# Pairing small matmuls on row halves, ending the norms' square sums on TensorE, and moving two low parts to VectorE

## The chip, the cores and the metric

The kernel runs on one core of a Trainium2 chip. The metric is the device time of one execution, in microseconds (us), as a median of runs; smaller is better. PE is TensorE (PEld its weight loads), DVE is VectorE, ACT is ScalarE, POOL is GpSimd, SP is SyncE.

## The reference, cut to what matters

256 tokens of width 1024 pass through two stacks of two layers. Everything is float32.

```python
def first_block(x, p, ...):
    for i in range(2):
        z = rmsnorm(x, norm_mix[i]) @ w_in[i]        # 14 pieces: queries, keys, values, gates ...
        y_a = nsa_mixer(...) @ w_up_nsa[i]           # compressed, selected and sliding-window keys
        y_b = retention(...) @ w_up_ret[i]
        x = x + (sigmoid(merge_a) * y_a + sigmoid(merge_b) * y_b) @ w_out[i]
        x = x + square(relu(rmsnorm(x, norm_mlp[i]) @ w_ff1[i])) @ w_ff2[i]
        x = x + sigmoid(rmsnorm(x, norm_ple[i]) @ w_ple_gate[i]) * (p[i] @ w_ple[i])

def rmsnorm(x, g):
    return x * rsqrt(mean(x * x, axis=-1) + 1e-6) * g

def second_block(x, ...):
    # layer 0: mixer_sb_ssm, then an MLP; layer 1: mixer_dsa, then an MLP; a layer norm behind each
    ...

def mixer_sb_ssm(x, w_in, ...):
    q, k, v, u = split(x @ w_in)                     # 8 heads of 64; u: 32 groups of 16 channels
    a_out = stick_breaking_attention(q, k, v)        # z = q k / 8; log sigmoids; a cumulative sum over keys
    y = s5_ssm(u, ...)                               # bu = u @ bbar (complex, 64 states a group), a scan, c @ x
    ...
    return concat(a_out, y) @ w_out
```

## The kernel before, in words

Each product of activations and weights is made of three fp32r matmuls: a high part times a high part, and each high part times the other's low part (`mm3`, L388 to L390; `paired`, L438 and L440, does it in two). Weights come in by DMA from one packed array (`raw`), ACT rounds them to the high part `hi` (L363) and DVE or POOL subtracts to get the low part `lo` (L366). The table `POOL` at the head of `_Env` says for which weight names POOL makes the first low part of a key; "ksw", the selected and sliding keys of the first stack, is in it, but only for layer 1 (`_split`).

A program writer issues the work in stages, with generators at the side (`_Env.add`, `step`, `run`): each step of the main work lets every generator in the side list take one step, up to its next `yield`. A scheduler then orders the instructions of each engine. It simulates a time line and may place an instruction of a later stage ahead of or between others; `e.behind((ins,))` keeps what stands in it behind an instruction. So the order on an engine isn't the order of the program text. PSUM banks come from two pools of four, "a" and "w"; a matmul that wants a bank has to wait until the reader of the bank's earlier use is through.

The parts that the change touches:

- **Norms** (`_Norm`; six of them in the first stack: mixer, MLP and PLE norm of each layer). The activations stand transposed, channels on partitions. For each of four slices of two channel groups, ACT squares 128x512 values (L516), and POOL (DVE for the first norm) adds them to a sum (L520); with slice 3 the two halves of the sum are folded into one (L522). `stats` then multiplies the 128x256 sum with a matrix of minus ones: two program matmuls of two columns, one for each half of the tokens (L532), which sums over the partitions. DVE and POOL's power function turn that into the factor `rc`, and a later matmul (L551) spreads it as `rb`. The products with the weights don't wait for it: the factor is applied when the results are read. In the PLE stage, POOL also scales x by `rb2` in four pieces (L694), and `stats` waits one step before its matmuls are issued.
- **Stick-breaking scores** (`stage_a`, `stage_b`, `side_attention` in `_second`). Heads 2j and 2j+1 stand on rows 0 to 63 and 64 to 127 of `kT` and `qT`. For one head at a time, `stage_a` multiplies a mask by a unit matrix into a bank (L1324, 128 rows), then two products of 64 rows (L1325, L1327); ACT makes three passes and DVE one (L1333). `stage_b` of the head before adds cumulative sums to the same bank (L1338, L1340, L1342).
- **State space inputs** (`_ssm_run`, L1887). For k = 0 to 3 and four quarters q, two program matmuls on 64 rows (rows 0 to 63 for even q, 64 to 127 for odd q) write one bank; DVE rotates it by cosines and sines, POOL combines, DVE scans. It is a generator at the side; it yields behind every second quarter.

## Time and profile before

| | |
|---|---|
| median of 3 runs | 1476.12 us (1475.64 to 1477.32) |
| profiled execution | 1473.14 us, of which the span is 1471.4 us |
| mean granted clock of TensorE | 0.993 of full speed |
| PE busy | 1435.8 us, 98% of the span |
| PEld busy | 1269.1 us |
| DVE, ACT, POOL busy | 1090.3, 784.9, 274.5 us |

The span runs from the first to the last instruction; 1.74 us of the profiled execution lie around it. PE's matmuls are pipelined, so that their busy times overlap; what one costs is read from the start of one to the start of the next. A row of the time line is: start, busy time, engine, line, operation, output and inputs, and in brackets the idle time before it with what ended it. "x4" in such a row means four machine instructions in a run; a float32 matmul (not fp32r) is two instructions for one of the program.

### The profile page before, as it was taken

To read this page: it belongs to the slowest core of one execution; us is meant where nothing else is said; L and a number is where in the kernel's file an instruction comes from. 1 tells how busy PE (TensorE), PEld (TensorE's weight loads), DVE (VectorE), ACT (ScalarE), POOL (GpSimd) and SP (SyncE) were. 2 spreads that over 40 slices of the span, in tenths; PEclk is the share of its full clock that TensorE was granted. 3 is DMA by queue.
4 is the path that set the end of the run, shared out by engine and by line. 5 is a ranking of instruction groups with operands and counts; after the bars stand their busy time and mean duration, and the time that the engine had idled before them with its cause. 6 is when DMAs were issued, how large, how long until landed. Compare 5 with 4: busy or idle time off the path is not lost.

```text
span 1471.4 us, 24711 instructions
## 1 busy us (share of the span) xinstructions
PE 1435.8 (98%) x9636; PEld 1269.1 (86%) x9636; DVE 1090.3 (74%) x1820; ACT 784.9 (53%) x1258; POOL 274.5 (19%) x201
## 2 busy tenths in 40 slices
PE   9999999999999999999999999999999998999997
PEld 6878999999998779999999998778888796788886
DVE  7796669666678696679877778877666688686666
ACT  6665545444556564455645555365444465654442
POOL 2343314000045343213000337510000100100000
PEclk9999999999999999999999999999999998999999
DMA  8553555655546653555565453336556362366551
GB/s 291 188 179 109 173 172 177 198 186 187 178 146 195 198 172 130 173 166 191 188 198 180 154 185 122 101 129 216 192 181 198 123 220 75 100 208 193 186 190 69
DMA packets 70677, 250.66 MB, mean 170 GB/s; under 512 B 8096, under 2 KB 8480, under 8 KB 70560
## 3 DMA queue, kind: packets, MB, share of 16 engines
q1 hardware_dynamic: 70560, 249.07, 51.6%
q8 instruction: 76, 1.25, 0.3%
q14 instruction: 41, 0.34, 0.1%
HBM read 247.99 MB, written 1.05 MB: 169 GB/s over the span
## 4 chain that ended last, share of the span: by engine, by line
PE 49%; DVE 4%; issue 1%; ACT 1%; POOL 0%; DVEq 0%; POOLq 0%
PE psw L438 11%; PE psa L388 9%; PE psa L390 9%; PE psa L389 9%; PE psw L440 6%; DVE lo L366 1%; DVE b L1896 1%; PE psw L2033 1%; PE psw L389 0%; PE psw L2019 0%; PE psw L390 0%; ACT b L1607 0%; PE psw L1887 0%; PE psw L388 0%; DVE b L1984 0%
## 5 line engine op out<-in xcount | busy, mean ns | idle before, releaser
L366 DVE TENSOR_TENSOR lo<-raw,hi 128x1024 fp32r<-128x1024 f32 (+1 forms) x409 | 512.5, 1260 | 216.7 <-ACT hi L363 215.9
L363 ACT ACTIVATE hi<-raw 128x1024 fp32r<-128x1024 f32 (+1 forms) x448 | 465.7, 1047 | 386.8 <-issue 141.4
L438 PE MATMUL psw<-act,hi 128*128 128x512 f32 x960 | 340.7, 397 | 0.0
L440 PE MATMUL psw<-act,lo 128*128 128x256 f32 x960 | 268.0, 281 | 0.0
L438 PEld LDWEIGHTS psw<-act,hi 128*128 128x128 f32 x960 | 179.9, 188 | 41.0
L440 PEld LDWEIGHTS psw<-act,lo 128*128 128x128 f32 x960 | 181.5, 189 | 1.7
L390 PE MATMUL psa<-b,lo 128*128 128x256 f32 x640 | 180.5, 283 | 0.0
L389 PE MATMUL psa<-b,hi 128*128 128x256 f32 x640 | 180.2, 283 | 0.0
L388 PE MATMUL psa<-b,hi 128*128 128x256 f32 x640 | 177.8, 283 | 0.0
L388 PE MATMUL psa<-act,hi 128*128 128x256 f32 x456 | 132.2, 291 | 0.0
L390 PE MATMUL psa<-act,lo 128*128 128x256 f32 x456 | 130.3, 286 | 0.5 <-DVE lo L366 0.5
L389 PE MATMUL psa<-act,hi 128*128 128x256 f32 x456 | 130.8, 287 | 0.0
L366 POOL TENSOR_TENSOR lo<-raw,hi 128x1024 fp32r<-128x1024 f32 x39 | 96.0, 2461 | 173.7 <-ACT hi L363 158.9
L389 PE MATMUL psa<-lo,act 128*128 128x512 f32 (+2 forms) x320 | 121.6, 383 | 3.6 <-DVE lo L366 2.6
L388 PE MATMUL psa<-hi,act 128*128 128x512 f32 (+2 forms) x320 | 122.3, 390 | 1.6 <-ACT hi L363 1.2
L390 PEld LDWEIGHTS psa<-b,lo 128*128 128x128 f32 x640 | 122.1, 191 | 0.1
L389 PEld LDWEIGHTS psa<-b,hi 128*128 128x128 f32 x640 | 122.0, 191 | 0.0
L388 PEld LDWEIGHTS psa<-b,hi 128*128 128x128 f32 x640 | 120.5, 191 | 1.2
L390 PE MATMUL psa<-hi,act 128*128 128x512 f32 (+2 forms) x320 | 117.9, 382 | 0.0
L388 PE MATMUL psa<-hi,b 128*128 128x512 f32 x256 | 99.7, 391 | 0.0
L389 PE MATMUL psa<-lo,b 128*128 128x512 f32 x256 | 99.6, 390 | 0.0
L390 PE MATMUL psa<-hi,b 128*128 128x512 f32 x256 | 98.7, 389 | 0.0
(360 smaller groups left out, 2692.2 us busy)
## 6 DMA issues: line engine op xcount, KB each, us to landing
raw<-in_ws_dram SPq DMA_DIRECT2D x450, 512.0 KB, 4.1
b<-in_ln_dram SPq DMA_DIRECT2D x8, 512.0 KB, 5.1
raw<-in_ws_dram SPq DMA_DIRECT2D x8, 280.0 KB, 3.7
raw<-in_ws_dram SPq DMA_DIRECT2D x4, 264.0 KB, 2.7
b<-in_x_dram SPq DMA_DIRECT2D x4, 256.0 KB, 5.0
out_dram<-b SPq DMA_DIRECT2D x4, 256.0 KB, 2.0
cb<-in_cb_dram SPq DMA_DIRECT2D x1, 676.0 KB, 7.1
b<-in_p_dram SPq DMA_DIRECT2D x2, 256.0 KB, 5.0
```

The source lines that it names most:

```text
L363: self.nc.scalar.activation(out=hi, in_=w, func=AF.Copy)
L366: eng.tensor_tensor(out=lo, in0=w, in1=hi.bitcast(F32), op=ALU.subtract)
L388: mm(out=out, lhsT=lh, rhs=rh, start=start, stop=False, skip_group_check=shared)
L389: mm(out=out, lhsT=lh, rhs=rl, start=False, stop=False, skip_group_check=shared)
L390: self.mlast = mm(out=out, lhsT=ll, rhs=rh, start=False, stop=stop, skip_group_check=shared)
L438: mm(out=bank.rearrange("p (v t) -> p v t", v=2), lhsT=h[:, c], rhs=act[2][k], start=k == 0, stop=False, skip_group_check=True)
L440: mm(out=bank[:, :256], lhsT=l[:, c], rhs=act[0][k], start=False, stop=k == len(hi) - 1, skip_group_check=True)
L1896: V.tensor_tensor_scan(out=xs[:, q, c], data0=mt[:, q], data1=w[:, q, c], initial=0.0, op0=ALU.mult, op1=ALU.add)
L2033: PE.matmul(out=o[64 * gg:64 * gg + 64, q0:256], lhsT=vw[:, kt, v0:v0 + 64], rhs=pts[s - 1 + gg][:, 256 * kt:256 * kt + 256 - q0], start=k ...
```

## The change

Four edits.

1. "ksw" leaves the table `POOL`, so both low parts of these keys in layer 1 are made by DVE, as those of layer 0 were.
2. The squares of slice 3 are no longer added to the sum and the fold is gone. The sum of slices 0 to 2 and the squares of slice 3, each with two halves, are four operands for `stats`, which accumulates them with four matmuls for each half of the tokens: eight program matmuls of two columns instead of two. In the PLE stage `stats` waits two steps instead of one, and POOL's four scalings of x stand behind the last of the norm's adds.
3. `stage_a` takes both heads of a pair: the products of the two row halves alternate in two banks, the mask matmuls come last. `side_attention` issues the two `stage_b` behind it, one step later.
4. The state space inputs take two quarters together, on opposite row halves, alternating in two banks.

```diff
-    POOL = {"rv": 1, "rg": 1, "ma": 1, "mb": 1, "up": 1, "su": 1, "glu": 1, "sv": 1, "ksw": 1}
+    POOL = {"rv": 1, "rg": 1, "ma": 1, "mb": 1, "up": 1, "su": 1, "glu": 1, "sv": 1}
...
-            pool = n < self.POOL.get(key[0], 0) and key[:2] != ("ksw", 0)
-            eng = self.nc.gpsimd if pool else self.nc.vector
+            eng = self.nc.gpsimd if n < self.POOL.get(key[0], 0) else self.nc.vector
...
-        if self.sum is None:
-            self.sum = sq
+        if c in (0, 3):
+            self.sum = [self.sum, sq] if c else sq
         else:
-            eng.tensor_tensor(out=self.sum, in0=self.sum, in1=sq, op=ALU.add)
-        if c == 3:
-            eng.tensor_tensor(out=self.sum[:, 0], in0=self.sum[:, 0], in1=self.sum[:, 1], op=ALU.add)
+            self.added = eng.tensor_tensor(out=self.sum, in0=self.sum, in1=sq, op=ALU.add)
...
         for T in range(2):
-            PE.matmul(out=ps[:, 2 * T:2 * T + 2], lhsT=self.sum[:, 0, 128 * T:128 * T + 128], rhs=K["negones"][:, :2])
+            for n in range(4):
+                PE.matmul(out=ps[:, 2 * T:2 * T + 2], lhsT=self.sum[n // 2][:, n % 2, 128 * T:128 * T + 128],
+                          rhs=K["negones"][:, :2], start=n == 0, stop=n == 3)
...
-        st = norm.stats("a", rs["prior"], wait=1)
+        st = norm.stats("a", rs["prior"], wait=2)
         e.add(st)
-        for b in range(4):
-            k = slice(2 * b, 2 * b + 2)
-            G.tensor_tensor(out=xT[:, k], in0=xT[:, k], in1=rs["rb2"], op=ALU.mult)
+        with e.behind((norm.added,)):
+            for b in range(4):
+                k = slice(2 * b, 2 * b + 2)
+                G.tensor_tensor(out=xT[:, k], in0=xT[:, k], in1=rs["rb2"], op=ALU.mult)
...
-    def stage_a(s):
-        j, g = s // 2, s % 2
-        hs = slice(64 * g, 64 * g + 64)
-        ps = e.bank()
-        diag = ps[:, :].rearrange("p (a q) -> p a q", a=4)[:, 0:4:2]
-        PE.matmul(out=diag, lhsT=im[:, 0], rhs=smask2, start=True, stop=False, skip_group_check=True)
-        PE.matmul(out=ps[:, 0:256], lhsT=kT[hs, j, 0:128], rhs=qT[hs, j, :], start=False, stop=False,
-                  skip_group_check=True)
-        PE.matmul(out=ps[:, 256:384], lhsT=kT[hs, j, 128:256], rhs=qT[hs, j, 128:256], start=False, stop=False,
-                  skip_group_check=True)
...
+    def stage_a(j):
+
+        pss = [e.bank() for _ in range(2)]
+        for o, n in ((0, 128), (256, 256)):
+            for g in range(2):
+                hs = slice(64 * g, 64 * g + 64)
+                PE.matmul(out=pss[g][:, o:o + 384 - n],
+                          lhsT=kT[hs, j, n - 128:n], rhs=qT[hs, j, n - 128:256], start=o == 0, stop=False,
+                          skip_group_check=True)
+        for g in range(2):
+            diag = pss[g].rearrange("p (a q) -> p a q", a=4)[:, 0:4:2]
+            PE.matmul(out=diag, lhsT=im[:, 0], rhs=smask2, start=False, stop=False, skip_group_check=True)
...
     def side_attention():
-        ready, lag = [], 1
-        for s in range(8 + lag):
-            while s >= 4 and "qk" not in D:
+        ready = []
+        for j in range(4):
+            while j >= 2 and "qk" not in D:
                 yield
-            if s < 8:
-                stage_a(s)
-            if s >= lag:
-                stage_b(s - lag)
-                if (s - lag) % 2:
-                    ready.append((s - lag) // 2)
+            stage_a(j)
             yield
-            if ready and "v" in D:
-                stage_c(ready.pop(0))
+            for g in range(2):
+                stage_b(2 * j + g)
+                if ready and "v" in D:
+                    stage_c(ready.pop(0))
+            ready.append(j)
+            yield
...
         for q in range(4):
-            h = slice(64 * (q % 2), 64 * (q % 2) + 64)
-            ps = e.bank()[:, :256].rearrange("p (c j) -> p c j", c=2)
-            for c in range(2):
-                PE.matmul(out=ps[:, c], lhsT=S["bT"][h, c, 2 * k + q // 2], rhs=up[h, k, q // 2])
+            if q % 2 == 0:
+                pss = [e.bank()[:, :256].rearrange("p (c j) -> p c j", c=2) for _ in range(2)]
+                for c in range(2):
+                    for n in range(2):
+                        h = slice(64 * n, 64 * n + 64)
+                        PE.matmul(out=pss[n][:, c], lhsT=S["bT"][h, c, 2 * k + q // 2], rhs=up[h, k, q // 2])
+            ps = pss[q % 2]
```

Because lines move, L520 is L519 afterwards, L532 is L530, L1887 is L1892, and the first of three split matmuls (L388) is L387.

How the instructions of an engine stand in a row was compared at three places. First PE at the state space inputs. Names such as psw_10494 are PSUM banks, "x2" are two program matmuls in a run. Before, the last two quarters of k = 2 stood next to each other:

```order
L390 MATMUL psa_10469<-hi_10323,act_9765 128x512
L1887 MATMUL psw_10494<-b_1691_10035,b_1487_8648 128x128 x2
L1887 MATMUL psw_10505<-b_1691_10035,b_1487_8648 128x128 x2
L388 MATMUL psa_10468<-hi_10327,act_9773 128x512
L389 MATMUL psa_10468<-lo_10328,act_9773 128x512
L1324 MATMUL psw_10516<-b_1683_9995 128x2x128
L1325 MATMUL psw_10516<-b_1680_9992,b_1681_9993 128x256
L1327 MATMUL psw_10516<-b_1680_9992,b_1681_9993 128x128
```

Afterwards, the same quarters:

```order
L1892 MATMUL psw_10523<-b_1691_10059,b_1487_8668 128x128 x2
L387 MATMUL psa_10498<-hi_10356,act_9797 128x512
L388 MATMUL psa_10498<-lo_10357,act_9797 128x512
L389 MATMUL psa_10498<-hi_10356,act_9797 128x512
L387 MATMUL psa_10497<-hi_10356,act_9797 128x512
L388 MATMUL psa_10497<-lo_10357,act_9797 128x512
L1892 MATMUL psw_10524<-b_1691_10059,b_1487_8668 128x128 x2
L1342 MATMUL psw_10419<-b_1761_10431,cb_7527 128x256
```

Five matmuls of another product stand between the two quarters. Over all eight pairs, four are adjacent before and one afterwards; that one is followed by a head's scores:

```order
L1892 MATMUL psw_10255<-b_1691_10059,b_1487_8668 128x128
L1892 MATMUL psw_10256<-b_1691_10059,b_1487_8668 128x128
L1892 MATMUL psw_10255<-b_1691_10059,b_1487_8668 128x128
L1892 MATMUL psw_10256<-b_1691_10059,b_1487_8668 128x128
L1325 MATMUL psw_10277<-b_1680_10016,b_1681_10017 128x256
L1325 MATMUL psw_10277<-b_1680_10016,b_1681_10017 128x128
L1330 MATMUL psw_10277<-b_1683_10019 128x2x128
L387 MATMUL psa_10226<-act_9879,hi_10124 128x256
```

The other head of the pair (psw_10278) comes ten rows later; none of the four pairs of heads stands together.

Second, POOL at the PLE norm of layer 0 (b_5 is x, b_758 the sum of squares). Before:

```order
L694 TENSOR_TENSOR b_5_96<-b_5_96,b_514_2843 128x512
L520 TENSOR_TENSOR b_758_4519<-b_758_4519,b_760_4527 128x512
L694 TENSOR_TENSOR b_5_96<-b_5_96,b_514_2843 128x512
L520 TENSOR_TENSOR b_758_4519<-b_758_4519,b_762_4536 128x512
L694 TENSOR_TENSOR b_5_96<-b_5_96,b_514_2843 128x512
L520 TENSOR_TENSOR b_758_4519<-b_758_4519,b_764_4545 128x512
L694 TENSOR_TENSOR b_5_96<-b_5_96,b_514_2843 128x512
L522 TENSOR_TENSOR b_758_4519<-b_758_4519 128x256
L603 TENSOR_TENSOR rc_4668<-rc_4668,mhalf_128 128x2
```

Afterwards:

```order
L519 TENSOR_TENSOR b_758_4527<-b_758_4527,b_760_4535 128x512
L519 TENSOR_TENSOR b_758_4527<-b_758_4527,b_762_4544 128x512
L694 TENSOR_TENSOR b_5_96<-b_5_96,b_514_2851 128x512 x4
L602 TENSOR_TENSOR rc_4717<-rc_4717,mhalf_128 128x2
L519 TENSOR_TENSOR b_802_4825<-b_802_4825,b_805_4837 128x512
```

The adds now stand ahead of all four scalings, an add and the fold are gone, and the power function (L602) stands behind the scalings as before. On PE, the statistics of this norm stand 24 program matmuls of the gate's product later than before.

Third, PE at the first norm, while the first weights arrive (psa_213 to psa_216 are banks of the first product). Before, the statistics came 26 rows behind these:

```order
L390 MATMUL psa_215<-hi_148,act_152 128x280
L390 MATMUL psa_216<-hi_148,act_152 128x280
L388 MATMUL psa_215<-hi_167,act_157 128x280
L388 MATMUL psa_216<-hi_167,act_157 128x280
L389 MATMUL psa_215<-lo_168,act_157 128x280
```

Afterwards:

```order
L389 MATMUL psa_214<-hi_148,act_152 128x280
L530 MATMUL psw_291<-ones_64,b_27_178 128x2 x2
L530 MATMUL psw_291<-ones_64,b_30_186 128x2 x2
L530 MATMUL psw_291<-ones_64,b_27_178 128x2 x2
L530 MATMUL psw_291<-ones_64,b_30_186 128x2 x2
L387 MATMUL psa_213<-hi_167,act_157 128x280
L387 MATMUL psa_214<-hi_167,act_157 128x280
L388 MATMUL psa_213<-lo_168,act_157 128x280
```

The statistics moved in between two weight parts.

## Rows read from the trace of the kernel before

**Rows 1.** The page: span's busy times, and the group of DVE's low parts

```profile
PE 1435.8 (98%) x9636; PEld 1269.1 (86%) x9636; DVE 1090.3 (74%) x1820; ACT 784.9 (53%) x1258; POOL 274.5 (19%) x201
...
L366 DVE TENSOR_TENSOR lo<-raw,hi 128x1024 fp32r<-128x1024 f32 (+1 forms) x409 | 512.5, 1260 | 216.7 <-ACT hi L363 215.9
```

**Rows 2.** Waits of PE: total us, times, longest us

```profile
PE psa L532 <- POOL b L522: 4.0, 2, 2.1
...
PE psa L389 <- DVE lo L366: 2.6, 3, 1.7
PE psw L1338 <- DVE b L1333: 2.2, 3, 1.0
...
PE psa L389 <- POOL lo L366: 0.9, 1, 0.9
```

**Rows 3.** Time line of PE, an MLP norm's statistics; columns as told above

```profile
660.18 0.40 PE L438 MATMUL psw<-act,hi 128*128 128x512 f32 x1
660.42 0.28 PE L440 MATMUL psw<-act,lo 128*128 128x256 f32 x1
660.53 0.50 PE L532 MATMUL psw<-ones,b 128*128 128x2 f32 x4
660.90 0.48 PE L438 MATMUL psw<-act,hi 128*128 128x512 f32 x1
661.21 0.28 PE L440 MATMUL psw<-act,lo 128*128 128x256 f32 x1
```

**Rows 4.** Time line of PE, the PLE norm's statistics of layer 0

```profile
417.17 0.61 PE L532 MATMUL psa<-ones,b 128*128 128x2 f32 x4 [2.05 <-POOL b L522]
```

**Rows 5.** Time line of POOL ahead of those statistics

```profile
413.25 2.20 POOL L694 TENSOR_TENSOR b<-b,b 128x512 f32<-128x512 f32 x1 [1.95 <-DVE act L484]
415.42 1.70 POOL L522 TENSOR_TENSOR b<-b 128x256 f32<-128x256 f32 x1
```

**Rows 6.** Time line of PE, start of layer 1

```profile
440.47 0.50 PE L389 MATMUL psa<-lo,act 128*128 128x512 f32 x1 [0.94 <-POOL lo L366]
...
444.36 0.50 PE L389 MATMUL psa<-lo,act 128*128 128x512 f32 x1 [1.73 <-DVE lo L366]
```

**Rows 7.** Time line of POOL, start of layer 1

```profile
437.78 5.44 POOL L366 TENSOR_TENSOR lo<-raw,hi 128x1024 fp32r<-128x1024 f32 x2 [0.22 <-ACT hi L363]
```

**Rows 8.** Time line of DVE, start of layer 1

```profile
438.98 1.99 DVE L706 SCALAR_TENSOR_TENSOR b<-b,b 128x512 f32<-128x512 f32 x1
440.89 3.42 DVE L366 TENSOR_TENSOR lo<-raw,hi 128x1024 fp32r<-128x1024 f32 x1
```

**Rows 9.** Time line of PE near the start

```profile
10.70 0.29 PE L390 MATMUL psa<-hi,act 128*128 128x280 f32 x1
12.19 0.52 PE L388 MATMUL psa<-hi,act 128*128 128x280 f32 x2 [1.20 <-ACT hi L363]
13.37 0.40 PE L389 MATMUL psa<-lo,act 128*128 128x280 f32 x1 [0.66 <-DVE lo L366]
```

**Rows 10.** Time lines of DVE and ACT near the start

```profile
10.59 0.68 DVE L520 TENSOR_TENSOR b<-b,b 128x512 f32<-128x512 f32 x1
...
10.97 0.61 ACT L516 ACTIVATE b<-b 128x512 f32<-128x512 f32 x1
```

**Rows 11.** Two stretches: us, busy of PE, PEld, DVE, ACT, POOL; clock; DMA

```profile
13.92:17.33 3.41, 3.41 (x15) 3.21 (x15) 2.79 (x4) 1.51 (x2) 0.00 (x0) 0.50 1.03 403
...
885.00:945.00 60.00, 57.83 (x409) 47.40 (x408) 53.98 (x85) 28.21 (x45) 41.72 (x43) 1.00 0.31 99
```

**Rows 12.** Time line of PE, state space inputs: one quarter, then two adjacent

```profile
892.96 0.28 PE L390 MATMUL psa<-act,lo 128*128 128x256 f32 x1
893.17 0.71 PE L1887 MATMUL psw<-b,b 64*128 64x128 f32 x4
893.81 0.39 PE L388 MATMUL psa<-act,hi 128*128 128x256 f32 x1
894.03 0.28 PE L389 MATMUL psa<-act,hi 128*128 128x256 f32 x1
...
896.16 0.72 PE L1887 MATMUL psw<-b,b 64*128 64x128 f32 x8
896.81 0.38 PE L1324 MATMUL psw<-b 128*128 128x256 f32 x1
```

More of the change, by code (lines that the diff above doesn't have):

```diff
@@ L502, in __init__ @@
         self.K, self.g = K, g
-        self.sum = self.rc = self.rb = None
+        self.sum = self.rc = self.rb = self.added = None
     def slice(self, xT, c):
@@ L1317, in _second @@
     sc, ws = {}, {}
-    def stage_a(s):
-        j, g = s // 2, s % 2
-        hs = slice(64 * g, 64 * g + 64)
-        ps = e.bank()
-        diag = ps[:, :].rearrange("p (a q) -> p a q", a=4)[:, 0:4:2]
-        PE.matmul(out=diag, lhsT=im[:, 0], rhs=smask2, start=True, stop=False, skip_group_check=True)
-        PE.matmul(out=ps[:, 0:256], lhsT=kT[hs, j, 0:128], rhs=qT[hs, j, :], start=False, stop=False,
-                  skip_group_check=True)
-        PE.matmul(out=ps[:, 256:384], lhsT=kT[hs, j, 128:256], rhs=qT[hs, j, 128:256], start=False, stop=False,
-                  skip_group_check=True)
-        l = e.t("b2", [128, 384])
-        A.activation(out=l, in_=ps[:, :384], func=AF.Abs)
-        A.activation(out=l, in_=l, func=AF.Exp, scale=-1.0)
-        A.activation(out=l, in_=l, func=AF.Ln, bias=1.0)
-        V.scalar_tensor_tensor(out=l, in0=ps[:, :384], scalar=0.0, in1=l, op0=ALU.max, op1=ALU.add)
-        sc[s] = (ps, l)
+    def stage_a(j):
[10 more added lines that the diff above has]
+        for g in range(2):
+            ps = pss[g]
+            l = e.t("b2", [128, 384])
+            A.activation(out=l, in_=ps[:, :384], func=AF.Abs)
+            A.activation(out=l, in_=l, func=AF.Exp, scale=-1.0)
+            A.activation(out=l, in_=l, func=AF.Ln, bias=1.0)
+            V.scalar_tensor_tensor(out=l, in0=ps[:, :384], scalar=0.0, in1=l, op0=ALU.max, op1=ALU.add)
+            sc[2 * j + g] = (ps, l)
     def stage_b(s):
@@ L1362, in side_attention @@
     def side_attention():
-        ready, lag = [], 1
-        for s in range(8 + lag):
-            while s >= 4 and "qk" not in D:
+        ready = []
+        for j in range(4):
+            while j >= 2 and "qk" not in D:
                 yield
-            if s < 8:
-                stage_a(s)
-            if s >= lag:
-                stage_b(s - lag)
-                if (s - lag) % 2:
-                    ready.append((s - lag) // 2)
-            yield
-            if ready and "v" in D:
-                stage_c(ready.pop(0))
+            stage_a(j)
+            yield
+            for g in range(2):
+                stage_b(2 * j + g)
[3 more added lines that the diff above has]
+            yield
         while ready:
```

## The prediction

> **What bounds the kernel now.** I read the page's busy times first: PE is busy 1435.8 us of a span of 1471.4 us and no other engine comes near it [rows 1]. So the order of PE's instructions and the few places where PE stands still decide the time, and a part of the change counts by what it does to PE's steps. Next I read the list of what PE waited for [rows 2]. Four of its entries lie where the change works: the square sums' statistics wait for the folded sum on POOL twice, 4.0 us in all; weight parts waited for DVE 2.6 us and once for POOL 0.9 us; the second stage of the stick-breaking scores (L1338) waited three times, 2.2 us. Then I read the time line of PE at each place, where a row "x4" is four machine instructions of two program matmuls: an fp32 matmul is two instructions, and the time from one row's start to the next one's is what it costs PE. All sums below stand against the profiled execution, 1473.14 us; the three timed runs have a median of 1476.12 us, 2.98 us more, and I carry the difference of the sum over to the median.
>
> **Statistics of the norms, the price.** Before, a norm has two L532 matmuls, four instructions; now eight, sixteen instructions. In a stretch without a wait four take 0.37 us from 660.53 to 660.90, and the next L438 takes 0.31 us (660.90 to 661.21) where an ordinary one takes 0.24 us (660.18 to 660.42) [rows 3]: 0.44 us in all, 0.11 us each. Twelve more per norm are 12 x 0.11 = 1.33 us, and 8.0 us for six norms if nothing hides them. The Trainium skill ("TensorEngine Tiling (Array Packing)", section Instruction Overhead) says that a matmul has about 60 cycles of overhead, so that one column lasts as long as sixty; that would be 0.025 us for each of these two-column instructions, an estimate from that page, and 0.3 us instead of 1.33 us for the twelve. The row disagrees, 0.11 us each, with a 128x128 weight load in every one. Statistics that cost next to nothing are rival C.
>
> **MLP norms (two).** The sums are ready: adds and statistics stand in a stretch where PE does not wait [rows 3]. Nothing hides the 1.33 us there. Term: 2 x 1.33 = **+2.7 us**; +2.3 if each hides one 0.2 us step's worth of waiting that I don't see.
>
> **PLE norms (two).** PE idles 2.05 us ahead of L532, until POOL's fold L522 has ended [rows 4]; the second norm has the same wait (2 times, 4.0 us in all [rows 2]). On POOL the fold comes last, behind a 2.20 us scaling of x (L694) and itself 1.70 us [rows 5]. Now only two adds stand ahead of the statistics, the four scalings are behind them, the fold is gone, and the order puts 24 more program matmuls ahead of the statistics on PE. So the wait goes; what is late next is the last square on ACT, and that stands ahead of those 24 matmuls. The added 1.33 us stays, since it fills PE itself. POOL's power function on the statistics is now queued behind all four scalings, but POOL has an add and the 1.70 us fold less to do, so they end before 415.45, where the last scaling ended before [rows 5], and PE comes to the statistics only after that. Term: 2 x (1.33 - 2.03) = **-1.4 us**; if the wait came back behind the scalings, up to +2.7.
>
> **Mixer norm of layer 1 and the two sliding-key low parts.** At 440.47 PE waits 0.94 us for POOL's low part and at 444.36 again 1.73 us for DVE's [rows 6]. On POOL the two low parts take 5.44 us [rows 7], and beside them DVE is slow: 3.42 us for a low part whose mean is 1.26 us [rows 1], and 1.99 us for an L706 [rows 8]. With both low parts on DVE, POOL is quiet, DVE has 2 x 1.26 = 2.5 us more to do and wins back 3.42 - 1.26 = 2.2 us and a part of the 1.99 us. I take half of the 2.67 us of waits to remain, since DVE is still the one that hands PE its low parts here one after the other. Term: 1.33 - 1.4 = **-0.1 us**, between -1.4 (all waits gone) and +1.3 (all there).
>
> **Startup norm.** PE idles 1.20 us before 12.19 and 0.66 us before 13.37 [rows 9]. In the new order the sixteen instructions stand in that wait: the last needed add on DVE ends at 11.27 and the last square on ACT at 11.58 [rows 10], so they run from 11.3 to about 13.1. The two L388, 0.52 us busy together, then end their steps near 13.55 and L389 starts there instead of at 13.37, 0.18 us later; the four at 18.3 are gone, 0.44 us. That is -0.3 us. Behind the waits the granted clock fell to half (1.2 instead of 2.4 GHz) from 13.92 to 17.33, 3.41 us [rows 11], which costs half of that, 1.7 us. PE stood nearly still for 1.86 of the 3 us before; now it has statistics there. Waits of 2 us elsewhere [rows 4] were followed by no fall, so the rows don't settle whether it falls again; I take half. Term: -0.3 - 0.8 = **-1.1 us**, between +0.2 and -2.1.
>
> **State space inputs.** An isolated quarter (x4) costs PE, from 892.96 to 894.03, 1.07 us less the 0.24 us of the two matmuls around it, **0.83 us**; two quarters on opposite row halves that stand next to each other (x8) take 0.65 us from 896.16 to 896.81, where one alone takes 0.64 from 893.17 to 893.81 [rows 12]. So the second quarter of an adjacent pair is free. The code before issues quarter after quarter, but its order already has four of eight pairs adjacent; the changed code asks for pairs, but its order has one adjacent pair, and in seven the scheduler put other matmuls between the quarters. Groups to pay for: before 4 + 8 = 12, now 1 + 14 = 15. Term: 3 x 0.83 = **+2.5 us**; +1.5 if quarters beside other half-row matmuls save their way in or out.
>
> **Scores.** No two heads stand next to each other in the new order either; each head is two products on 64 rows and then the mask matmul. The same three matmuls cost the same. Twice a head follows directly on a quarter of the state space inputs, which are 64 rows too, and one way out and one way in (0.10 us each, the excess of 0.21 and 0.22 over 0.12 around x4 in [rows 12]) fall away: **-0.4 us**, between 0 and -0.6. The three waits of stage b, 2.2 us [rows 2], I leave as they are: the rows between a head's scores and its L1342 number 22 to 71 now, 23 to 71 before.
>
> **Sum**: +2.7 - 1.4 - 0.1 - 1.1 + 2.5 - 0.4 = **+2.2 us**, so 1475.3 us for a profiled execution like the one shown and **1478.3 us** for the median. A measurement here can tell about 0.2%, 2.95 us, from no change; so this is "same", nearer to the slower end. With its terms at their near bounds the forecast reaches from 1475 to 1481 us.
>
> **Rivals.**
>
> A. The waits all go: startup keeps its clock (-2.1), the layer boundary waits no more (-1.4), the stage b waits end because both heads' scores come early (-2.2), and the quarters save their ways (+1.5). With +2.7 - 1.4 - 0.6 the sum is -3.5 us: **1472.6 us**. For it: each of these waits has its releaser on DVE or POOL, which lose work there. Against it: four things must come together. Chance 0.22.
>
> B. Stage b becomes late. Both heads' scores are asked for at once, so six ACT passes and two DVE steps stand one after another, and the second head's L1342 comes while DVE, busy 53.98 of 60 us in this stretch [rows 11], is still behind; two scores and two quarters now hold all four banks of their pool until DVE has read them. It decides from the point where the PE work between a head's score and its L1342 is shorter than that chain, about 25 rows. Price: if all eight heads wait the longest wait seen, 1.0 us [rows 2], 8.1 us instead of 2.2, +5.9 us, the sum is +8.1: **1484.2 us**. For it: the waits exist already at 23 to 27 rows. Against it: the scheduler spread the heads. Chance 0.18.
>
> C. The twelve added instructions of a norm take PE no time, because their weight loads run beside the work ahead. Then 1.33 us goes from the terms of the MLP norms, the PLE norms and the boundary, five times, 6.7 us: sum -4.5 us, **1471.6 us**. The Trainium skill's overhead figure above points this way. The 0.37 us of four [rows 3] speaks against it. Chance 0.02. That the pairs really run as pairs, -3.3 instead of +2.5, would take another order than the one built; I give it no more than is in C.
>
> **How the numbers follow.** The forecast has 0.58, and of it 0.13 lies above 1479.07, the bound of slower; B adds 0.18, so slower has 0.31, same 0.45, and faster, from A and C, 0.24. The range reaches down to A and up towards B: 1472.5 to 1482.5 us; about 2 in 10 lie outside, most of them above.
>
> **What would show it.** Right: L530 in bursts of 0.11 us without idle time ahead of it at both PLE norms; one x8 and fourteen x4 groups of L1892, each x4 at 0.83 us; no POOL low part at the second layer's start and PE's waits there shorter than 2.67 us. Wrong: waits for L1342 of more than 4 us in all (B); a granted clock that stays full near 14 us together with no wait at the layer boundary and at L1342 (A); sixteen L530 in far less than 1.7 us (C).

## The result and the profile after

The changed kernel takes **1484.5 us** (median of 5 runs, 1480.8 to 1487.0), the kernel before 1476.1 us (5 runs, 1473.2 to 1477.3): ratio 1.0054, 95% interval 1.0037 to 1.0070. It is slower by 8 us; the forecast was 1478.3 us with a range up to 1482.5.

The profiled execution of the changed kernel took 1484.52 us, its span is 1482.7 us. It stands at the median, that of before stood 3 us under its own, so between the two traces lie 11.3 us. Both traces hold the same 8040 split matmuls (`mm3` and `paired`). The start of the n-th one after, less its start before, is how far the change has fallen behind by then:

| stretch (start in the trace before) | forecast, us | measured, us |
|---|---|---|
| startup, to 58 us | -1.1 | -0.5 |
| attention of layer 0, 70 to 82 us | 0 | +2.5, later -0.2 |
| two MLP norms (234, 662 us) | +2.7 | +1.0 and +1.0 |
| first PLE norm (417 us) | -0.7 | -1.0 |
| start of layer 1 (436 to 460 us) | -0.1 | -0.1 |
| attention of layer 1 | 0 | +0.3 |
| second PLE norm (848 us) | -0.7 | -0.9 |
| start of the second stack (867 to 869 us) | 0 | +1.5 |
| state space mixer and stick-breaking heads (881 to 978 us) | +2.1 | **+6.8** |
| the rest | 0 | +1.1 |

The PLE norms and the start of layer 1 went nearly as told, the MLP norms cost less. The time line of PE at the first norm answers [rows 9]; then the first PLE norm answers [rows 4], and the start of layer 1 [rows 6]:

```profile
11.27 1.95 PE L530 MATMUL psw<-ones,b 128*128 128x2 f32 x16 [0.33 <-DVE b L519]
13.08 0.50 PE L387 MATMUL psa<-hi,act 128*128 128x280 f32 x2
...
420.46 1.84 PE L530 MATMUL psa<-ones,b 128*128 128x2 f32 x16
422.17 0.36 PE L387 MATMUL psa<-act,hi 128*128 128x256 f32 x1
...
443.42 0.50 PE L388 MATMUL psa<-lo,act 128*128 128x512 f32 x1 [0.28 <-DVE lo L365]
445.29 0.40 PE L387 MATMUL psa<-hi,act 128*128 128x280 f32 x1 [0.44 <-ACT act L482]
```

Sixteen statistics take 1.71 us from 420.46 to 422.17, 0.107 us each; nothing waits ahead of them any more; at the start they run from 11.27 to 13.08, and L387 follows at 13.08. DVE's low part no longer takes 3.42 us [rows 8]: the two made here take 1.22 and 1.21 us, and POOL makes none beside them; PE's waits are 0.28 and 0.44 us instead of 2.67:

```profile
439.18 1.22 DVE L365 TENSOR_TENSOR lo<-raw,hi 128x1024 fp32r<-128x1024 f32 x1
440.31 1.92 DVE L483 SCALAR_TENSOR_TENSOR act<-b,prm,act 128x256 fp32r<-128x256 f32 x2
442.15 1.21 DVE L365 TENSOR_TENSOR lo<-raw,hi 128x1024 fp32r<-128x1024 f32 x1
```

The loss is in the mixer's stage. Its windows (columns as in [rows 11]), before and after, from the same split matmul to the same split matmul:

```profile
881.24:977.79 96.55, 93.96 (x685) 77.18 (x683) 79.92 (x124) 49.62 (x78) 48.97 (x50) 1.00 0.36 118
```

```profile
884.78:988.09 103.31, 97.19 (x684) 79.49 (x683) 80.29 (x125) 50.72 (x80) 49.13 (x50) 0.98 0.33 110
```

6.76 us more; DVE, ACT and POOL have nearly the same work as before, so they stand longer. PE idles 6.12 us (103.31 - 97.19) instead of 2.59. So 3.5 of the 6.76 us are idle time of PE, 1.7 are a fall of the clock (below), and 1.5 are PE's own work, for which the forecast had 2.1. The time line of PE after shows where it stands:

```profile
916.64 0.70 PE L1342 MATMUL psw<-b,cb 128*128 128x256 f32 x2 [2.40 <-DVE b L1337]
...
974.86 0.50 PE L387 MATMUL psw<-b,hi 128*128 128x256 f32 x2 [1.80 <-ACT b L463]
976.15 0.38 PE L388 MATMUL psw<-b,hi 128*128 128x256 f32 x1 [0.79 <-DVE b L464]
```

The first is the second stage (L1342) of the second head, 2.40 us where the three waits of that step before were 2.2 us in all [rows 2]. That head's max (L1337) stands on DVE behind four scans of the mixer, so DVE does not wait for ACT here. One of these scans takes 2.51 us, where the median of all 32 is 0.41, and beside it POOL makes a low part. DVE's time line, then POOL's:

```profile
912.03 4.11 DVE L1902 TENSOR_TENSOR_SCAN b<-b,b 128x128 f32<-128x128 f32 x4
916.06 0.53 DVE L1337 SCALAR_TENSOR_TENSOR b<-psw,b 128x384 f32<-128x384 f32 x1
```

```profile
912.33 2.47 POOL L365 TENSOR_TENSOR lo<-raw,hi 128x1024 fp32r<-128x1024 f32 x1
```

Before, four scans stood between two maxes in the same way, and PE waited 0.74 us there. The other two waits of PE are new: PE has nothing left to do until the output of the state space mixer has been through its gelu. That output is the end of a chain over PE, DVE and POOL, and it comes 73.9 us after the stage's first state space matmul, against 69.4 us before. Right behind these waits, from 976.70 to 980.10, the granted clock is 0.50 (1.2 instead of 2.4 GHz), which costs 1.7 us:

```profile
976.70:980.10 3.40, 3.40 (x18) 3.40 (x17) 0.53 (x1) 0.00 (x0) 0.00 (x0) 0.50 0.70 227
```

What DVE waited for from 887.7 to 965.4 us, and the two longest of these waits at the maxes, in its time line:

```profile
DVE b L1337 <- ACT b L1336: 5.2, 2, 3.1
DVE lo L365 <- ACT hi L363: 2.5, 2, 2.3
DVE b L1897 <- PE psw L1892: 2.4, 2, 1.3
DVE b L1864 <- PE psw L1862: 2.4, 1, 2.4
```

```profile
934.51 0.56 DVE L1337 SCALAR_TENSOR_TENSOR b<-psw,b 128x384 f32<-128x384 f32 x1 [3.06 <-ACT b L1336]
937.25 0.56 DVE L1337 SCALAR_TENSOR_TENSOR b<-psw,b 128x384 f32<-128x384 f32 x1 [2.17 <-ACT b L1336]
937.72 3.46 DVE L1902 TENSOR_TENSOR_SCAN b<-b,b 128x128 f32<-128x128 f32 x8
```

DVE stands 5.23 us at the maxes of the third pair of heads, which wait for ACT's passes, and eight scans of the mixer queue behind them. Before, DVE's waits for that step (L1333) were 0.9 us in all.

The quarters cost what was told. An isolated one is 898.15 to 898.79; the only pair runs as x8, with a head's scores (64 rows, too) right behind it:

```profile
898.15 0.71 PE L1892 MATMUL psw<-b,b 64*128 64x128 f32 x4
898.79 0.39 PE L387 MATMUL psa<-act,hi 128*128 128x256 f32 x1
...
899.70 0.71 PE L1892 MATMUL psw<-b,b 64*128 64x128 f32 x8
900.25 0.81 PE L1325 MATMUL psw<-b,b 64*128 64x256 f32 x4
```

The two places of the first stack that the forecast had at nothing: in the attention of layer 0 a wait that was 1.05 us before is 1.50 us, and the clock falls behind it, so that split matmuls step 0.43 instead of 0.23 us for 3.4 us:

```profile
78.31 0.61 PE L1059 MATMUL psw<-ca,b 128*128 128x128 f32 x3 [1.50 <-DVE b L1051]
...
81.23 0.63 PE L387 MATMUL psa<-hi,act 128*128 128x512 f32 x1
81.65 0.63 PE L388 MATMUL psa<-lo,act 128*128 128x512 f32 x1
...
82.47 0.39 PE L387 MATMUL psa<-hi,act 128*128 128x512 f32 x1
```

And at 870.03 PE waits 0.75 us for the last activations of the first stack. Their factor `rb` comes later now (L551 at 854.28 us before, L550 at 859.08 after); that this is the reason was not tested.

### The profile page after: what moved, and what is told of

Same layout as the page of the kernel before. It is cut to its first block, busy times and chain, and to the rows that moved or that the text cites. A ratio compares the mean times of both kernels' runs of the same rounds, so it can differ in the third digit from the quotient of the medians.

```text
span 1482.7 us, 24833 instructions
## 1 busy us (share of the span) xinstructions
PE 1446.2 (98%) x9708; PEld 1278.4 (86%) x9708; DVE 1084.7 (73%) x1820; ACT 785.3 (53%) x1258; POOL 252.0 (17%) x189
## 3 DMA queue, kind: packets, MB, share of 16 engines
HBM read 247.99 MB, written 1.05 MB: 168 GB/s over the span
## 4 chain that ended last, share of the span: by engine, by line
PE 87%; DVE 7%; ACT 2%; issue 2%; DMA 2%; POOL 0%; DVEq 0%; SPq 0%; ACTq 0%; POOLq 0%
PE psa L387 16%; PE psa L389 16%; PE psa L388 16%; PE psw L437 15%; PE psw L439 8%; PE psw L388 3%; PE psw L389 3%; PE psw L387 3%; DVE lo L365 1%; DMA raw<-in_ws_dram 1%; PE psw L1077 1%; DVE b L1902 1%; ACT hi L363 1%; PE psw L763 1%; PE psw L2039 1%
## 5 line engine op out<-in xcount | busy, mean ns | idle before, releaser
L365 DVE TENSOR_TENSOR lo<-raw,hi 128x1024 fp32r<-128x1024 f32 (+2 forms) x411 | 509.9, 1247 | 223.6 <-ACT hi L363 222.6
L388 PE MATMUL psa<-b,hi 128*128 128x256 f32 x640 | 180.2, 283 | 0.0
L387 PE MATMUL psa<-b,hi 128*128 128x256 f32 x640 | 177.8, 283 | 0.0
L388 PE MATMUL psa<-act,hi 128*128 128x256 f32 x456 | 130.4, 286 | 1.2 <-DVE act L464 1.0
L387 PE MATMUL psa<-act,hi 128*128 128x256 f32 x456 | 131.2, 289 | 0.0
L387 PE MATMUL psa<-hi,act 128*128 128x512 f32 (+2 forms) x320 | 123.0, 391 | 2.8 <-ACT hi L363 1.9
L388 PE MATMUL psa<-lo,act 128*128 128x512 f32 (+2 forms) x320 | 122.1, 384 | 0.6 <-DVE lo L365 0.5
L388 PEld LDWEIGHTS psa<-b,hi 128*128 128x128 f32 x640 | 122.0, 191 | 0.0
L387 PEld LDWEIGHTS psa<-b,hi 128*128 128x128 f32 x640 | 120.4, 190 | 1.2
L365 POOL TENSOR_TENSOR lo<-raw,hi 128x1024 fp32r<-128x1024 f32 x37 | 89.5, 2418 | 175.7 <-ACT hi L363 158.6
L387 PE MATMUL psa<-hi,b 128*128 128x512 f32 x256 | 99.6, 391 | 0.0
L388 PE MATMUL psa<-lo,b 128*128 128x512 f32 x256 | 99.6, 390 | 0.0
```

The costliest lines, as they stand in the source:

```text
L365: eng.tensor_tensor(out=lo, in0=w, in1=hi.bitcast(F32), op=ALU.subtract)
L387: mm(out=out, lhsT=lh, rhs=rh, start=start, stop=False, skip_group_check=shared)
L388: mm(out=out, lhsT=lh, rhs=rl, start=False, stop=False, skip_group_check=shared)
```

## The experiments

Medians are of 4 to 12 runs, each beside runs of the kernel before on the same chip (medians of those 1474.4 to 1475.8 us). "Stage" is the mixer's stage as above, in the one profiled execution: its length, PE's idle time in it, and how long the clock was at half. What "+" stands for is told in the text.

| kernel | edits | median, us | ratio to before (95%) | stage, us | PE idle | at half clock |
|---|---|---|---|---|---|---|
| before | | 1476.1 | | 96.6 | 2.6 | 0 |
| changed | 1 2 3 4 | 1484.5 | 1.0054 (1.0037 to 1.0070) | 103.3 | 6.1 | 3.4 |
| scores_only | 3 | 1479.9 | 1.0033 (1.0018 to 1.0048) | 101.4 | 6.6 | 6.8 |
| norm_only | 2 | 1483.0 | 1.0045 (1.0031 to 1.0059) | 99.7 | 3.4 | 6.8 |
| ssm_only | 4 | 1476.1 | 1.0001 (0.9988 to 1.0014) | 96.7 | 2.9 | 0 |
| norm_ksw | 1 2 | 1479.7 | 1.0032 (1.0020 to 1.0044) | 100.2 | 3.3 | 6.8 |
| no_scores | 1 2 4 | 1476.1 | 1.0002 (0.9991 to 1.0014) | 98.8 | 2.9 | 6.8 |
| scans_first | all, + | 1483.1 | 1.0046 (1.0028 to 1.0064) | 105.3 | 7.3 | 6.8 |
| scores_bank_a | all, + | 1478.0 | 1.0021 (1.0008 to 1.0034) | 104.2 | 5.6 | 13.7 |
| one_bank_a | all, + | 1479.9 | 1.0038 (1.0024 to 1.0051) | 99.8 | 9.0 | 3.4 |
| lag_pair | all, + | 1478.1 | 1.0019 (1.0008 to 1.0031) | 99.6 | 9.6 | 3.4 |
| after_no_max | all, + | 1474.4 | 1.0001 (0.9988 to 1.0014) | 94.9 | 5.0 | 0 |
| pairs_no_max | 3 4, + | 1472.5 | 0.9987 (0.9973 to 1.0001) | 94.3 | 5.6 | 3.4 |

PE's idle time sorts the kernels: it is 5.0 to 9.6 us in every one that takes the scores of two heads together, the two that only the text has (before_lag_pair 8.6, lag_no_max 7.8) included, and at most 3.4 us in all others. So taking them together does make PE wait; which chain it then waits for is the question of the rest.

### Which edit

Theory W: the maxes of two heads, which wait for ACT, hold up the scans on DVE. Rivals: Q, the quarters that the order took apart; N, the statistics.

**scores_only**, edit 3 of the diff alone.

> The kernel before with edit 3 alone (both heads' scores together). Theory W (the maxes of the two heads, which wait for ACT, stand on DVE ahead of the scans of the state space inputs and hold them up; the chain of the state space mixer ends late and PE waits for it): in this order, too, two maxes stand ahead of the eight scans of k = 2, so DVE waits some 4 to 5 us for ACT there and the time is about 1481 us, +4 to +6. Theory Q (the price is the quarters of the inputs that the order takes apart, 0.83 us each): twelve groups as before, so 1476 us, no change. Theory N (the price is the norms' statistics): no change.

Measured 1479.9 us. Four pairs of quarters stand together in its trace, as before, so Q has nothing to say for these 4 us (one later quarter stands in pieces among a head's scores). DVE waits 4.5 us for ACT ahead of two maxes, PE 2.57 us for L1342 and 1.79 + 0.76 us for the mixer's end. That is W's time and these are its waits; that the maxes are the reason for PE's waits is not shown by it.

**norm_only**, edit 2 alone.

> The kernel before with edit 2 alone (the norms' square sums). W: the first stack costs +1 to +3.5 us (0.97 us for each MLP norm, about 0 for the rest, 1.7 us if the clock falls once more), the second stack has one max ahead of the eight scans or none and doesn't change: 1477 to 1479.5 us. Q: eleven groups instead of twelve, -0.8 us in the second stack. N: 1482 us or more, most of the whole loss.

Measured 1483.0 us, far over W's figure and within N's (1482 us or more). The place speaks against N: by the table of split matmuls it has lost 5.9 us when the first stack ends. An MLP norm is 1.0 us of it each, the PLE norms gain 1.0 and 0.9, the start of the second stack costs 1.5, and the rest lies where the edit isn't: 2.1 us at 71 to 81 us, with a fall of the clock at 78.5, and 2.4 us between 453 and 593 us, in attention and MLP of layer 1. In the mixer's stage PE idles 3.4 us, 0.8 more than before, and the clock was at half for 6.8 us.

**no_scores**, all but edit 3.

> The changed kernel with edit 3 undone. W: no maxes of two heads ahead of the eight scans, so the second stack is as before: 1477 to 1479.5 us. Q: eleven groups instead of fifteen, so 3.3 us less than the changed kernel, 1481 us. N: no gain, 1484.5 us.

Measured 1476.1 us: the whole loss is gone with edit 3. Neither Q nor N gave that, and it lies under W's figure too. The prices do not add up: edit 3 alone costs 4 us, edits 1 and 2 cost 4 us (norm_ksw below), edits 1, 2 and 4 nothing, all four 8 us.

**scans_first**, the changed kernel and

```diff
-            V.scalar_tensor_tensor(out=l, in0=ps[:, :384], scalar=0.0, in1=l, op0=ALU.max, op1=ALU.add)
+            with e.behind((e.scan,) if j == 2 else ()):
+                V.scalar_tensor_tensor(out=l, in0=ps[:, :384], scalar=0.0, in1=l, op0=ALU.max, op1=ALU.add)
```

(`e.scan` is the last scan issued; the line that sets it is left out).

> The changed kernel with one thing more: the two maxes of the third pair of heads are kept behind the last scan issued before them, so that on DVE eight scans go first. W: DVE's 5.2 us of waiting for ACT there are gone, the mixer's chain ends 4 to 5 us earlier, PE's wait for it (2.6 us) and the fall of the clock behind it (1.7 us) go: 1479 to 1481 us. Q: fourteen groups instead of fifteen, 1483.7 us. N: no gain.

Measured 1483.1 us, a miss for W in this form. The waits at the maxes are gone, but others have come, as the list of DVE's waits says:

```profile
DVE b L1903 <- PE psw L1863: 6.2, 1, 6.2
DVE b L1898 <- PE psw L1893: 4.1, 2, 2.8
...
DVE b L1865 <- PE psw L1863: 2.4, 1, 2.4
```

PE's waits of 2.4 us for L1343 and 1.8 + 0.8 us at the end are all still there. The 2.4 us did not go: four scans stand ahead of the second head's max as before, one of them 2.51 us long again. So the maxes of the third pair are not the cause by themselves. My reading, not shown, is that the heads' chain (PE, ACT, DVE, PE, ACT) and the mixer's chain share the same engines in one fixed order, and what one doesn't wait for, the other does.

### Banks, and the norms once more

Theory P: edit 3 overfills the four banks of pool w. **scores_bank_a** takes both score banks from pool a, **one_bank_a** one of them:

```diff
-        pss = [e.bank() for _ in range(2)]
+        pss = [e.bank("a") for _ in range(2)]
...
+        pss = [e.bank("aw"[g]) for g in range(2)]
```

> The changed kernel with the two banks of the scores taken from pool a instead of w. Theory P (the pool of four banks is what edit 3 overfills: two scores and two quarters; so the order takes quarters apart and the mixer's chain ends late): seen from the order the quarters stand in pairs from the fifth on, 2 to 3 groups fewer of 0.83 us, the waits for the second stage and for the mixer's end fall below 1.5 us each: 1477 to 1479 us. Rival D (both heads' maxes and second stages coming together are the harm, whatever the banks): 1482 us or more.

> The changed kernel with one of the two banks of a pair of scores from pool a. The order has ten groups of quarters instead of the changed kernel's seventeen (as the trace counts them), and two maxes still stand ahead of the eight scans. Theory Q (the quarters taken apart are PE work, 0.83 us each): 4 to 6 us less than the changed kernel, 1478 to 1481 us, with PE's idle time in the stage as long as in the changed kernel (6 us). Rival D (maxes of two heads ahead of the scans): no gain, 1483 us or more.

1478.0 and 1479.9 us, 6.5 and 4.6 us less than the changed kernel (the profiled execution of scores_bank_a took 1481.5 us, with 13.7 us at half clock in the stage). With the other banks the order puts the quarters together (12 and 13 runs in the trace instead of 17, one quarter of the 17 being in three pieces). PE's idle time hardly fell in the first (5.6 us) and rose in the second (9.0), and the waits for L1342 stay at 2.6 us or more. So P is right in its first half, and Q has its share here: the banks made the order take the quarters apart, and this costs PE. The wait for the second stage is not made by the banks.

> The kernel before with edits 1 and 2. Theory K (the loss of edit 2 alone, 7 us, came from the sliding keys' stage, where POOL's slow low parts now meet a later norm, and goes with edit 1): 1475 to 1477 us. Rival N (the statistics themselves cost the 7 us): 1481 us or more.

**norm_ksw** gave 1479.7 us, between K and N. With both low parts on DVE the 2.4 us at 453 to 593 us of norm_only are gone. It differs from no_scores in the code of edit 4 only and is 3.6 us slower. Their profiled executions lie 6.6 us apart; of that 2.0 us come with a fall of the clock at 78 us, and 2.9 us lie beyond 1200 us, in the last layer, where no edit is.

> The kernel before with edit 4 alone. Theory O (the scheduler's order decides, and it has twelve groups of quarters, as before): 1476 us, within 1.5 us. Rival (pairs are made as written, four groups fewer): 1472.5 us.

**ssm_only**: 1476.1 us, O. Code that writes the quarters in pairs changes nothing as long as the order takes them as before.

**fold_mlp_mix** keeps the fold for three norms:

```diff
-        if c in (0, 3):
+        if c == 0 or c == 3 and not self.fold:
             self.sum = [self.sum, sq] if c else sq
```

> Edits 1 and 2, but with the fold and the two statistics matmuls kept for the MLP norms and for layer 1's mixer norm, so that PE ends the sums only at the first norm and the PLE norms. If the statistics cost PE time where nothing waits for POOL (1.0 to 1.3 us for each of three norms) and pay where PE waited for the fold: 2 to 3.5 us less than edits 1 and 2, 1473 us. Rival (the differences between these orders are other waits): no gain over edits 1 and 2.

1480.1 us (1.0033, 1.0021 to 1.0045), no gain over norm_ksw: in its trace the MLP norms' 1.0 us each are saved, and lost again behind a wait of 1.6 us at 458 us, one of 1.4 us in the attention of layer 1, and a fall of the clock at 13.7 us, where norm_ksw's trace has none.

### The chain

**lag_pair** asks for the second stages one pair later, and the pairs take their banks from pool a and w in turn; **before_lag_pair** does so without edits 1 and 2. The part that decides:

```diff
+        for j in range(5):
+            if j < 4:
+                stage_a(j)
+            if j:
+                for g in range(2):
+                    stage_b(2 * j - 2 + g)
...
```

> The changed kernel with the second stages one pair later than the scores, so that ACT and DVE have the next pair's scores to work on meanwhile; scores take their banks from pool a and w in turn. Ten groups. Theory W2 (PE's 2.4 us for the first second stage and 2.6 us for the mixer's end come from second stages asked for right behind their scores): the wait for L1342 falls below 1 us, the rest of the stage is like the one-bank kernel: 1475 to 1478 us. Rival (the waits only move): 1479 us or more, idle time in the stage 5 us or more.

> The kernel before with edit 4 and the lagged pairs, without edits 1 and 2. The norms keep the fold, so the first stack is that of the kernel before; the second stack has ten groups. W2: 1473 to 1475.5 us, a little below the kernel before. Rival: as the waits of scores_only, 1478 us or more.

1478.1 and 1479.5 us (1.0026, 1.0013 to 1.0039): the second is the rival's figure; the first lies between the two, with the rival's idle time. The order is the densest of all, ten or eleven runs of quarters, and PE is busy only 89.98 us of lag_pair's 99.58, 4 us less than before, yet the stage is 3 us longer:

```profile
PE psw L1861 <- DVE b L1916: 4.0, 2, 3.7
PE psa L1342 <- DVE b L1337: 2.6, 1, 2.6
PE psa L1415 <- ACT b L1349: 1.5, 1, 1.5
```

What PE saves, it waits; of the 3 us, 1.7 are the half clock. So theory C: the chains over DVE and ACT set this stage. To take work off them without touching PE's, the softplus was written as ln(1 + exp z) instead of max(z, 0) + ln(1 + exp -|z|), which computes the same as long as exp z stays in range:

```diff
-            A.activation(out=l, in_=ps[:, :384], func=AF.Abs)
-            A.activation(out=l, in_=l, func=AF.Exp, scale=-1.0)
+            A.activation(out=l, in_=ps[:, :384], func=AF.Exp)
             A.activation(out=l, in_=l, func=AF.Ln, bias=1.0)
-            V.scalar_tensor_tensor(out=l, in0=ps[:, :384], scalar=0.0, in1=l, op0=ALU.max, op1=ALU.add)
```

> The changed kernel with the scores' softplus taken as ln(1 + exp z) straight away: two ACT passes a head instead of three, and no max on DVE (eight of 0.5 us, and their waits for ACT). The result is the reference's. Theory C (the stage of the state space mixer is set by the mixer's chain over DVE, POOL and ACT, not by PE; work that PE saves there turns into waits, and these let the clock fall): the chain loses 3.9 us of DVE work and the 5.2 us of waits ahead of it, so the stage gets 5 to 8 us shorter: 1476 to 1479 us. Theory E (PE's own work sets the stage): only the 2.4 us wait for L1342 goes, 1482 us.

**1474.4 us**, 10 us less than the changed kernel, and more than C asked for. The stage, and the scores in the time line of PE:

```profile
881.76:976.63 94.87, 89.88 (x684) 75.78 (x683) 80.70 (x117) 46.37 (x72) 49.40 (x50) 1.00 0.36 119
```

```profile
910.34 0.92 PE L1325 MATMUL psw<-b,b 64*128 64x256 f32 x8
911.19 0.50 PE L1330 MATMUL psw<-b 128*128 128x256 f32 x2
```

The mixer's last output comes 66.8 us after the stage's first state space matmul instead of 73.9, PE no longer waits for it, and the clock does not fall behind it. So far C holds. But PE's idle time fell by 1.1 us only, to 4.99, since it now waits elsewhere (2.6 us at the quarters, 1.3 us at L1355). Of the 8.4 us that the stage is shorter, 5.6 are PE's own work and 1.7 the half clock: the new order has three of the four pairs of heads together (one as x8 above, two with pieces of a quarter between them), the changed kernel has none. E's 1482 us counted on the same work of PE. So this run shows that the mixer's end and the fall of the clock behind it hang on the heads' passes in this order; it does not decide between C and E for the stage as a whole.

> The kernel before with the same softplus without a max. C and E: PE's three waits for L1338 (2.2 us) go, little more can, since PE's own work fills 94 of the 96.5 us of the stage: 1473 to 1474.5 us. If it gains over 4 us, neither holds.

> The kernel before with the softplus without a max once more, in more rounds, for its interval: 0.1% under the kernel before, 1472.5 to 1474.5 us.

1473.4 us (0.9990, 0.9977 to 1.0003) and again 1473.6 us (0.9991, 0.9979 to 1.0003): the three waits for L1338 are gone, as C and E said.

> The kernel with the lagged pairs and the softplus without a max. C: of its 9.6 us of idle time in the stage 4 us or more go, and no fall of the clock there: 1472 to 1475 us. E: 1477 us or more, since PE's work there is the same.

> The changed kernel without edit 3, with the softplus without a max. C: the 2.0 us wait and the fall of the clock at 909 us, which cost 5.4 us together, mostly go: 1471 to 1474 us. E: 1475 to 1476 us.

1477.2 us (1.0012, 1.0000 to 1.0023) and 1475.8 us (1.0006, 0.9993 to 1.0018): misses for C, and both are E's figures. In both, the wait for one step of the mixer's chain on DVE stays (L1916 in lag_pair, L1914 without the max; 3.72 and 2.02 us), with a fall of the clock; the heads don't decide that one. Taking the max away takes 1.8 us off PE's idle time in lag_pair's stage, 1.4 in that of before, 1.1 in that of the changed kernel, and nothing in that of no_scores.

> The kernel before with edits 3 and 4 and the softplus without a max, without edits 1 and 2. By theory C the stage of the mixer is as long as in after_no_max (95 us) or a little shorter, and the first stack has no dearer statistics: 1471 to 1474 us. If the clock falls in the stage, as in no_scores_no_max, 1475 to 1477 us.

**pairs_no_max**: 1472.5 us, the lowest median of all, 0.9987 with an interval that just reaches 1. It keeps the pairs of edits 3 and 4 and drops edits 1 and 2. Against before_no_max_again, which ran beside it, it is 1.1 us, which these runs cannot tell from nothing.

## Why the prediction was wrong

- **The mixer's stage** is the step that failed. The sum there was of PE's work: +2.5 for the quarters, -0.4 for the scores, and "the three waits of stage b, 2.2 us [rows 2], I leave as they are", from counts of rows between a head's scores and its L1342. The two work terms held (+1.5 us measured for +2.1), and so did the waits of stage b in all (2.40 us for 2.2). What the sum put at nothing is that PE would run out of work before the mixer's last output: 2.59 us of waiting there, 0.7 us at two smaller waits for DVE, and 1.7 us of half clock right behind. That is +6.8 instead of +2.1. What the forecast should have asked is when the stage's other engines are through: [rows 11] had DVE busy 54 of 60 us, and the output that PE waits for comes 4.5 us later (73.9 us after the first state space matmul, for 69.4). In after_no_max, with two passes a head on ACT and no max on DVE, it comes at 66.8 us and this wait and the fall are gone. Why the order makes that chain late is shown only in part: the maxes of the third pair hold up eight scans, but scans_first takes that away without a gain. The long scans beside POOL's low parts are a rival that no run tests.
- **Rival B** gave 1484.2 us against 1484.5 measured, with a chance of 0.18, and the right stage. The nearness of the number is luck: its price was eight waits of 1 us for L1342, and its own sign, more than 4 us of these in all, did not come (2.4 us). Of the 9.2 us that part the traces from the forecast, half lie outside this stage. A second head's L1342 did come while DVE was behind, as B says, but that costs no more than before. That banks are short was right for the order of the quarters, not for the waits.
- **The quarters**: right in kind. 0.83 us for an isolated one is what the trace shows, and scores_bank_a and one_bank_a gain when they stand together again.
- **The scores**: "the same three matmuls cost the same" could hold only as no pair ran together. Where pairs do (scores_only, after_no_max), 8 instructions start in the time of 4.
- **MLP norms**: mis-sized, +1.0 instead of +1.33 us each, the same in every kernel with edit 2 that has no fold there. Two of the sixteen stand 3 us ahead of the other fourteen, among other matmuls, where PE had 0.16 us of waiting before; that the 0.3 us come from there is not shown. The overhead that the Trainium skill gives for a matmul ("TensorEngine Tiling (Array Packing)", section Instruction Overhead) would have made it 0.3 us, an estimate; the trace has 0.107 us per instruction, and so rival C fell.
- **PLE norms**: -1.0 and -0.9 instead of -0.7 each, right. The second one gives 1.5 us back at the start of the second stack, which I had not asked: there the next product waits for the last activations. Every kernel with edit 2 shows these 1.5 us. What the sum also left out is a fall of the clock that may follow the first of these waits: of the seven profiled executions without edit 2 six have one at 415 to 420 us, all but the one that the forecast was made from; of the twelve with edit 2 none has.
- **Startup and start of layer 1**: within their bounds, -0.5 (for -1.1) and -0.1 us. The clock did fall again at 14.1 us in this execution; in the profiled executions of no_scores and scans_first it did not, and these gain 2.3 us at the start. Half was the honest term.
- **Other places**: +2.5 us at 70 to 82 us and +1.1 us in the last layer had no term. The edits don't touch them. Whether the scheduler's order moved them or the execution did was not separated: two executions of one kernel (before_no_max) differ by 1.5 us in the startup and by 0.8 us in the attention of layer 1.
- **Rival A** fell: the waits at the layer boundary and at the PLE norms went or shrank, but the clock fell at the start, and stage b kept its 2.4 us.

## What to carry to other kernels

An engine that is 98% busy bounds the kernel on the whole, not each stage; ahead of a sum of its steps, ask in each stage which engine would be next and when the last output of its chain comes. Work that two partners issue together on half the array saves PE's time only where the order leaves them together, and the saving is lost again where the engines behind them are late: lag_pair has 4 us less of PE's work in the stage than before and 7 us more of waiting. And an order that a scheduler makes anew for each edit comes out with other waits and other falls of the clock hundreds of microseconds from the edit, 1 to 4 us in these traces: a term for these belongs in the range of every such forecast.

## What the runs showed of the hardware

- Matmuls on the two row halves run at the same time, of both kinds here: eight instructions of two quarters start in the time of four [rows 12], those of two heads' scores too (0.85 us to the next row, 910.34 to 911.19 in after_no_max, and 0.85 us for one head, 902.37 to 903.22 in the changed kernel), and a quarter's four and a head's four do so with each other (0.86 us together from 944.21 in the changed kernel, in pieces of one and two).
- The mixer's scans on DVE are slow beside a low part that POOL makes. In each of the 19 traces every scan that lasts over 1 us (1.26 to 2.63 us) overlaps one; scans beside a quiet POOL take about 0.4 us. Two of these long scans stand in the mixer's stage of every kernel, three in most, and no run here moved the low part away from them.
- The clock's falls differ between executions of one kernel. Two executions of the kernel of before_no_max have nearly the same PE work and the same idle time (1.2 us) in the mixer's stage. In the second one the clock fell to half at 923.9 us for 6.8 us, and its stage is 97.2 us instead of 94.0. Their windows around the place, first one, then the other:

```profile
920.00:925.00 5.00, 4.23 (x21) 3.06 (x20) 5.00 (x9) 1.06 (x1) 3.64 (x5) 1.00 0.00 0
```

```profile
920.00:925.00 5.00, 4.22 (x19) 2.93 (x18) 5.00 (x11) 1.06 (x1) 3.63 (x7) 0.89 0.05 13
```

- This may be much of the spread of the runs. The mean granted clock of a run tells what it lost at most: 1 less the clock, times the span (a fall while PE stands still costs nothing). In the mean of its runs the kernel before loses 11.8 us so, the changed kernel 13.6 us, scores_only 16.9 us (the clock is given to 0.001, which is 1.5 us in one run); without it the means stand at 1463.4, 1470.2 and 1463.7 us. By this reading the loss of scores_only is the clock's, which falls behind PE's new waits, and 6.8 of the changed kernel's 8.6 us in the mean are waits and PE work.
